# Output projections of a two-layer trunk by seven block products per pair of tiles, with weight sums made in DRAM

## The chip, the cores and the metric

One core of one Trainium2 chip runs the whole program. The metric is device time in microseconds (us) for one execution. The engines are named as in the profile: PE (matmul), PEld (weight load), DVE (vector), ACT (scalar), POOL (GpSimd) and SP, whose queue issues most of the DMAs.

## The reference

Two layers are computed over 16 learned meta tokens followed by 512 tokens, so 528 columns, with 1024 features. In each layer:

```python
h = rmsnorm(h_res, norm_gain[l])
proj = h @ w_in[l]        # u_pool, z_pool, c_q, c_kv, k_rope, z_mla, g_pool, g_mla
y_pool = (pool_mix(u_pool, ...) * silu(z_pool)) @ pool_w_up[l]
o_mla  = mla(c_q, c_kv, k_rope, pos, ...)          # latent attention, 8 heads
y_mla  = (o_mla * silu(z_mla)) @ mla_w_up[l]
merged = sigmoid(g_pool) * y_pool + sigmoid(g_mla) * y_mla
h_res  = h_res + merged @ w_out[l]
```

The output is `h_res` without the meta tokens. The change concerns the last line, a product of a 1024 x 1024 matrix with 1024 features by 528 columns (512 in the last layer, where the meta tokens are no longer needed).

## The kernel before

Activations are kept transposed: features on the 128 partitions, tokens along the free dimension. A matrix of 1024 outputs is worked in 8 tiles of 128 outputs, and the 1024 inputs of each tile in 8 blocks of 128. Every float32 operand is split into a high part in the rounded format float32r and a low remainder, and each block is three matmuls: high by high, low activation by high weight, and high activation by low weight (`mm3`, lines 184 to 187).

All plain projections stand in one list, `plan`, built by `register`. `stream` walks through it as a generator: it loads weights four chunks of 512 columns ahead (`wload`: SP loads a `raw` tile, of which there are three, ACT makes the high part `whi` on line 180, DVE the low part `wlo` on line 181), emits the matmuls, and calls an evacuation routine for each finished PSUM tile. The layer's own code, `go`, calls `upto(name)` to run the list as far as a named projection, and `gap` or `fill` to put a stretch of these matmuls between the steps of attention, so that PE has work while a head's softmax is on its way. After the program is written in this order, the tile framework's scheduler sets the final order on each engine.

In layer 0 a projection has two column segments of 264, in layer 1 one of 512. PSUM has four tiles `mm` for projections and three tiles `S`, which attention uses for its scores.

The stages around the change:

- `gm0` to `gm7`: the gates of the attention branch, kept in slots `cq0` to `cq7`.
- `mu0` to `mu7`: the up projection of the attention branch. `ev_mu` multiplies by the gate on DVE from PSUM (line 882), adds the pooling branch `am`, which lives in the tile `xb`, on POOL (line 884), and splits the sum into high and low on ACT and DVE (lines 276 and 277). The result is `mg[m]`, in the buffers `hh`/`hl` which also hold the normalised input of a layer.
- `o0` to `o7`: the output projection. `ev_o` loads the residual of the tile by SP, computes 0.5 x PSUM + residual on DVE (line 898), and stores it: to the output in the last layer, otherwise into `xb`, with a copy to the DRAM tensor `scr` (from which the last layer loads its residual) and a square for the next norm.
- After `o7` of layer 0, `split_h` makes the next layer's `hh`/`hl` from `xb` (lines 336 and 338).

The evacuation of the output projection before:

```python
sp.dma_start(xr[:, a:b], xT[:, m, a:b])
dve.scalar_tensor_tensor(out=xn[:, a:b], in0=ps, scalar=0.5, in1=xr[:, a:b], op0=ALU.mult, op1=ALU.add)
sp.dma_start(scr[:, m, a0 - NM:b - NM], xn[:, a0:b])
if b == T:
    nxt.square_x(m)
```

Of the kernel before, what the change touches and what calls it, by code (L numbers as in the profile page):

```python
# [9 lines left out]
F32 = mybir.dt.float32  # L10
# [61 lines left out]
def trunk(ctx, tc, xT, pos, win, wkr, wqb, wkb, wvb, wgr, wpu, wmu, wout, gains, const, yT):  # L72
# [44 lines left out]
    def rawt():  # L117
        return wp.tile([P, 512], F32, tag="raw", name=nm("raw"), bufs=3)
# [48 lines left out]

    loads = [0]
# [15 lines left out]
    def mm3(out, wh, wl, xh, xl, start, stop):  # L184
        pe.matmul(out, wh, xh, start=start, stop=False)  # L185
        pe.matmul(out, wh, xl, start=False, stop=False)  # L186
        newest[0] = pe.matmul(out, wl, xh, start=False, stop=stop)  # L187
# [5 lines left out]
    def stream():  # L193
# [3 lines left out]
        def load(i):  # L197
            g_, c = flat[i]
            n = min(512, g_.width - c)
            return wload(g_.src[:, c:c + n], n, g_.gain, g_.spare)  # L200
# [109 lines left out]

    hbuf = [(slot(f"hh{k}", F32R), slot(f"hl{k}", F32R)) for k in range(8)]

    class Layer:
        def __init__(self, l):
            self.l, self.last = l, l == DEPTH - 1
            self.XS = XTOK if self.last else FULL
            self.x0 = NM if self.last else 0
            self.xt = xt if l == 0 else [None] * 8
# [7 lines left out]
            self.sq = []  # L326
            self.st = self.acc = self.inv = self.cinv = self.kraw = self.kp = None
# [13 lines left out]
        def square_x(self, k):  # L341
            self.xsq[k] = slot(f"cq{4 + k}" if k < 4 else f"q{k}")
# [534 lines left out]
        def ev_mu(self, m):  # L877
            def ev(ps, a, b):
                if a == self.x0:
                    self.mg[m] = self.hs[m]  # L880
                t = tmp()
                dve.scalar_tensor_tensor(out=t[:, :b - a], in0=self.gms[m][:, a:b], scalar=1.0, in1=ps,  # L882
                                         op0=ALU.add, op1=ALU.mult)
                gp.tensor_add(t[:, :b - a], t[:, :b - a], self.am[m][:, a:b])  # L884
                split(*self.mg[m], t[:, :b - a], a, b)
            return ev

        def ev_o(self, m, nxt):
            def ev(ps, a, b):
                xr = tmp()  # L890
                if self.last:
                    sp.dma_start(xr[:, a:b], scr[:, m, a - NM:b - NM])
                    xn = xr
                else:
                    sp.dma_start(xr[:, a:b], xT[:, m, a:b])
                    nxt.xt[m] = xb[:, m]
                    xn = nxt.xt[m]
                dve.scalar_tensor_tensor(out=xn[:, a:b], in0=ps, scalar=0.5, in1=xr[:, a:b],
                                         op0=ALU.mult, op1=ALU.add)
                a0 = max(a, NM)  # L900
                if self.last:
                    sp.dma_start(yT[:, m, a - NM:b - NM], xn[:, a:b])
                    return
                sp.dma_start(scr[:, m, a0 - NM:b - NM], xn[:, a0:b])
                if b == T:
                    nxt.square_x(m)
            return ev

        def register(self, nxt):
# [52 lines left out]
            for m in range(8):  # L962
                add(f"mu{m}", wmu[l, m], 512, evac=self.ev_mu(m), xs=lambda: self.ogs, segs=XS)
                plan[-1].spare = m % 2 == 1
            mg = lambda: self.mg
            for m in range(8):
                add(f"o{m}", wout[l, m], D, evac=self.ev_o(m, nxt), xs=mg,
                    segs=[(NM, NM + SEQ // 2), (NM + SEQ // 2, T)] if self.last and m == 7 else XS)
# [4 lines left out]
        def go(self, nxt):  # L973
# [13 lines left out]
            self.norm_sums()  # L987
            up("u1")
# [22 lines left out]
            for h in range(H):  # L1011
# [4 lines left out]
                self.pv(prev, (2, 3))  # L1016
                prev = kn_
# [6 lines left out]
            self.pv(prev, (2, 3))  # L1024
            up("gm7")
            flush()
            if not self.last:
                for p in range(4):
                    self.meta_out(p)
            up("o7")  # L1030
# [79 lines left out]
```

## Time and profile before

| what | value |
|---|---|
| timed runs (median; lowest to highest of 3) | 789.21 us; 789.16 to 789.3 |
| profiled execution, first to last instruction (span) | 787.1 us |
| median of the timed runs less that span | 2.1 us |
| granted PE clock | 1.000 |
| PE, DVE, ACT, POOL busy in the span | 780.9, 535.1, 410.8, 194.4 us |
| `mu` and `o` of layer 0, first matmul to first matmul of what follows | 332.4 to 356.4, 356.4 to 403.3 us |
| `mu` and `o` of layer 1 | 716.6 to 739.1, 739.1 to 783.8 us |

The profile is of one execution. The span is what its instructions cover; no separate total is listed for that execution, so the median of the timed runs stands beside it. In the rows of the profile, a line such as "L181 DVE TENSOR_TENSOR wlo<-raw,whi" names the line of the kernel, the engine, the operation, and what it writes and reads by the program's names without buffer numbers. Matmuls overlap, so the duration of one is longer than the distance to the next.

### The profile page before, as it was taken

What the parts mean: (1) busy time and instruction counts of PE and PEld (TensorE: products, weight loads), DVE (VectorE), ACT (ScalarE), POOL (GpSimd) and SP (SyncE); (2) the same over time, 40 slices, a digit from 0 to 9 for tenths busy, and PEclk for the clock granted to TensorE, in tenths of its full rate; (3) what the DMA queues carried; (4) which work ended last, traced back from release to release, by engine and by line L of the source; (5) the groups of instructions that cost most, each with busy time, mean ns of one, the idle gap of its engine ahead of it and who ended that gap; (6) DMA issues with size and microseconds to landing.
All of it is one profiled execution on the core that took longest, in us unless ns stands there. A gap on an engine that the chain in (4) does not pass through costs nothing.

```text
span 787.1 us, 14567 instructions
## 1 busy us (share of the span) xinstructions
PE 780.9 (99%) x5301; PEld 708.6 (90%) x5301; DVE 535.1 (68%) x1165; ACT 410.8 (52%) x930; POOL 194.4 (25%) x259
## 2 busy tenths in 40 slices
PE   9999999999999999999999999999999999999998
PEld 8999899999999999999997898887788888887887
DVE  5848787446779987675464487775467888755932
ACT  7645655635656565633354356455445666554420
POOL 1034504002333242051000145131022333410500
PEclk9999999999999999999999999999999999999999
DMA  6242333423223212224642422334232222122372
GB/s 242 82 102 85 96 120 102 128 81 94 96 76 92 78 58 78 95 81 146 192 123 94 95 88 90 129 88 136 96 105 88 95 84 82 65 81 67 102 242 84
DMA packets 52263, 81.83 MB, mean 104 GB/s; under 512 B 8784, under 2 KB 17360, under 8 KB 52192
## 3 DMA queue, kind: packets, MB, share of 16 engines
q1 hardware_dynamic: 52048, 80.65, 32.9%
q8 instruction: 41, 0.67, 0.4%
q14 instruction: 30, 0.25, 0.1%
q10 hardware_dynamic: 144, 0.26, 0.1%
HBM read 74.49 MB, written 4.27 MB: 100 GB/s over the span
## 4 chain that ended last, share of the span: by engine, by line
PE 95%; DMA 2%; DVE 1%; issue 1%; ACT 0%; SPq 0%; ACTq 0%
PE mm L185 28%; PE mm L187 28%; PE mm L186 28%; PE mm L796 2%; PE S L186 2%; PE S L187 1%; PE S L185 1%; PE o L802 1%; PE o L801 1%; PE S L453 1%; DMA xb<-xT 1%; PE mm L355 1%; DVE wlo L181 1%; PE mm L412 0%; DMA rinv<-win 0%
## 5 line engine op out<-in xcount | busy, mean ns | idle before, releaser
L185 PE MATMUL mm<-hh,whi 128*128 128x264 f32 (+2 forms) x1096 | 346.7, 318 | 0.2 <-ACT racc L810 0.2
L186 PE MATMUL mm<-hl,whi 128*128 128x264 f32 (+2 forms) x1096 | 343.9, 315 | 0.0
L187 PE MATMUL mm<-hh,wlo 128*128 128x264 f32 (+2 forms) x1096 | 343.0, 315 | 0.0
L181 DVE TENSOR_TENSOR wlo<-raw,whi 128x512 fp32r<-128x512 f32 (+2 forms) x251 | 188.6, 755 | 119.6 <-ACT whi L180 115.9
L180 ACT ACTIVATE whi<-raw 128x512 fp32r<-128x512 f32 (+2 forms) x251 | 150.4, 601 | 187.5 <-PE mm L186 126.5
L185 PEld LDWEIGHTS mm<-hh,whi 128*128 128x128 f32 x1096 | 205.9, 188 | 13.6 <-ACT racc L810 0.5
L186 PEld LDWEIGHTS mm<-hl,whi 128*128 128x128 f32 x1096 | 206.6, 189 | 11.8
L187 PEld LDWEIGHTS mm<-hh,wlo 128*128 128x128 f32 x1096 | 205.5, 188 | 12.0
L774 POOL TENSOR_TENSOR pm<-pa,rs 128x16 f32<-128x16 f32 x32 | 11.6, 361 | 181.3 <-DVE rs L769 181.3
L560 POOL TENSOR_TENSOR racc<-racc,tmp 128x264 f32<-128x264 f32 (+1 forms) x15 | 14.2, 948 | 153.8 <-ACT tmp L559 129.8
L702 POOL TENSOR_TENSOR tmp<-kp,bc 64x528 f32<-64x528 f32 x16 | 22.5, 1408 | 76.9 <-PE mm L675 44.5
L884 POOL TENSOR_TENSOR tmp<-tmp,xb 128x264 f32<-128x264 f32 (+1 forms) x24 | 27.1, 1149 | 58.2 <-DVE tmp L882 33.1
L730 DVE CUSTOM_DVE_ANT_0 S<-S,maskw,nqs 128x272 f32<-128x272 f32 (+4 forms) x80 | 38.5, 498 | 4.2 <-PE S L187 3.9
L737 ACT ACTIVATE cq<-S,bia 128x400 f32<-128x400 f32 (+2 forms) x48 | 24.6, 516 | 22.6 <-DVE bia L764 12.0
L185 PE MATMUL mm<-u,whi 128*128 128x264 f32 (+1 forms) x108 | 35.2, 326 | 0.0
L187 PE MATMUL mm<-cq,wlo 128*128 128x264 f32 (+1 forms) x108 | 34.5, 323 | 0.7 <-DVE wlo L181 0.7
L187 PE MATMUL mm<-u,wlo 128*128 128x264 f32 (+1 forms) x108 | 34.8, 323 | 0.0
L185 PE MATMUL mm<-cq,whi 128*128 128x264 f32 (+1 forms) x108 | 34.6, 320 | 0.0
L186 PE MATMUL mm<-cq,whi 128*128 128x264 f32 (+1 forms) x108 | 34.5, 321 | 0.0
L277 DVE TENSOR_TENSOR tl<-mm,th 128x512 fp32r<-128x512 f32 (+1 forms) x64 | 29.3, 481 | 6.1 <-ACT th L276 5.1
L776 POOL TENSOR_TENSOR cq<-cq,rs 128x384 f32<-128x384 f32 (+1 forms) x32 | 32.8, 1025 | 0.0
L186 PE MATMUL mm<-kn,whi 128*128 128x264 f32 (+1 forms) x96 | 30.7, 321 | 0.0
(252 smaller groups left out, 1362.4 us busy)
## 6 DMA issues: line engine op xcount, KB each, us to landing
raw<-win SPq DMA_DIRECT2D x143, 256.0 KB, 2.6
raw<-wout SPq DMA_DIRECT2D x32, 256.0 KB, 2.7
bc<-kdr SPq DMA_DIRECT2D x16, 264.0 KB, 3.6
raw<-wpu SPq DMA_DIRECT2D x16, 256.0 KB, 2.7
raw<-wmu SPq DMA_DIRECT2D x16, 256.0 KB, 2.5
raw<-wqb SPq DMA_DIRECT2D x12, 256.0 KB, 2.6
tmp<-xT SPq DMA_DIRECT2D x16, 132.0 KB, 3.0
tmp<-scr SPq DMA_DIRECT2D x7, 256.0 KB, 3.4
```

Of the source, the lines that this page charges most:

```text
L180: act.activation(hi[:, :n], raw[:, :n], AF.Copy)
L181: dve.tensor_sub(lo[:, :n], raw[:, :n], hi[:, :n].bitcast(F32))
L185: pe.matmul(out, wh, xh, start=start, stop=False)
L186: pe.matmul(out, wh, xl, start=False, stop=False)
L187: newest[0] = pe.matmul(out, wl, xh, start=False, stop=stop)
L277: dve.tensor_sub(lo[:, a:b], src, hi[:, a:b].bitcast(F32))
L702: gp.tensor_mul(kf[r0:r0 + 64, :], self.kp[r0:r0 + 64, :], bc[r0:r0 + 64, :])
L730: dve.tensor_tensor_reduce(out=sv, in0=sv, in1=mask, scale=nqs[:, i, h:h + 1], scalar=3e38, op0=ALU.add, op1=ALU.min, accum_out=bia[:, c:c ...
L737: act.activation(pv, sv, AF.Exp, scale=-1.0, bias=bia[:, i:i + 1], accum_out=rs[:, c:c + 1])
L776: gp.tensor_mul(pt[i][:, NM:], pt[i][:, NM:], rs[:, i:i + 1].to_broadcast([P, n - NM]))
L796: pe.transpose(tr[:, P * (i - j):P * (i - j + 1)], pt[i][:, NM + P * j:NM + P * (j + 1)], ident)
L884: gp.tensor_add(t[:, :b - a], t[:, :b - a], self.am[m][:, a:b])
```

## The change

The output projection is done by Strassen's scheme in Winograd's form. The 1024 inputs are taken as two halves (tiles 0 to 3 and 4 to 7), the columns as two halves (`XH`: 264 and 264 in layer 0, 256 and 256 in layer 1), and the outputs as four pairs of tiles. For each pair, eight products of four blocks become seven, numbered `p` in the code: three use plain activations (`p` 1, 2, 3), four use mixed ones (4 to 7). Of the weights, three products take a plain half tile of `wout` and four take a sum, kept in a new DRAM tensor `wsum`.

- `ev_mu` keeps its result unsplit in `f`, makes high and low halves of what plain products need (`halves`, with the factor 0.5), and for each pair of tiles k and k + 4 `mixed` makes the activation sums on DVE and POOL and splits them.
- `weight_sums` is called once per head step: SP copies four half tiles from `wout` to `wsum` in DRAM, and POOL adds to them with accumulating DMAs. The first DMA of each group waits for the newest matmul.
- `residual` loads the residual into `xb` right after the `mu` of a tile; products are added there on DVE, or copied to SBUF by ACT and added by POOL where one product goes to several places.
- The order of products is written out in `out_body` (`head` + `rest`). The `mu` tiles go in the order 0, 4, 1, 5, 2, 6, 3, 7.
- The copy of layer 0's result to `scr` is written after `cq1` of layer 1. There are five `raw` tiles, and squares of layer 1 use other slots.

```diff
-        return wp.tile([P, 512], F32, tag="raw", name=nm("raw"), bufs=3)
+        return wp.tile([P, 512], F32, tag="raw", name=nm("raw"), bufs=5)
...
+    wsum = [[dp.tile([P, 4, 512], F32, name=f"wsum{l}{u}") for u in range(4)] for l in range(DEPTH)]
...
             def ev(ps, a, b):
-                t = tmp()
-                dve.scalar_tensor_tensor(out=t[:, :b - a], in0=self.gms[m][:, a:b], scalar=1.0, in1=ps,
-                                         op0=ALU.add, op1=ALU.mult)
-                gp.tensor_add(t[:, :b - a], t[:, :b - a], self.am[m][:, a:b])
-                split(*self.mg[m], t[:, :b - a], a, b)
+                t = self.f[m]
+                hi = T if m >= 4 else mid
+                for c, d in self.XH:
+                    if a <= c and d <= b:
+                        dve.scalar_tensor_tensor(out=t[:, c:d], in0=self.gms[m][:, c:d], scalar=1.0, in1=ps[:, c - a:d - a],
+                                                 op0=ALU.add, op1=ALU.mult)
+                        gp.tensor_add(t[:, c:d], t[:, c:d], self.am[m][:, c:d])
+                        if d == hi:
+                            self.halves(self.mg[m], t, self.x0, hi)
+                if b == T:
+                    if m >= 4:
+                        self.mixed(m - 4)
...
+        def halves(self, hl, t, a, b):
+            act.activation(hl[0][:, a:b], t[:, a:b], AF.Copy, scale=0.5)
+            dve.scalar_tensor_tensor(out=hl[1][:, a:b], in0=t[:, a:b], scalar=0.5, in1=hl[0][:, a:b].bitcast(F32),
+                                     op0=ALU.mult, op1=ALU.subtract)
+
+        def mixed(self, k):
...
+            dve.tensor_sub(w[:, b:c], u[:, b:c], w[:, b:c])
+            gp.tensor_sub(u[:, b:c], u[:, a:b], u[:, b:c])
+            dve.tensor_sub(u[:, a:b], u[:, a:b], w[:, b:c])
+            self.halves(self.tt[k][0:2], u, a, c)
+            gp.tensor_sub(w[:, a:b], w[:, a:b], u[:, a:b])
+            self.halves(self.tt[k][2:4], w, a, c)
...
+            head = [(p, u) for u in range(3) for p in (1, 3, 2)]
+            rest = [(6, 0), (5, 0), (7, 0), (6, 1), (4, 0), (5, 1), (7, 1), (6, 2), (4, 1), (5, 2), (7, 2), (1, 3), (4, 2),
+                    (6, 3), (2, 3), (5, 3), (7, 3), (3, 3), (4, 3)]
...
+                for k in range(4):
+                    xs = self.mg[k + o] if p < 4 else self.tt[k][o:o + 2]
+                    c = P * k
+                    mm3(ps, w[0][:, c:c + P], w[1][:, c:c + P], xs[0][:, a:b], xs[1][:, a:b],
+                        k == 0 and p not in (2, 7, 4), k == 3, True)
...
+                if p == 1:
+                    self.q1[u] = q = sqt()
+                    act.activation(q[:, :n], ps, AF.Copy)
+                    gp.tensor_add(x12, x12, q[:, :n])
+                    gp.tensor_sub(x22, x22, q[:, :n])
+                    gp.tensor_sub(x21, x21, q[:, :n])
+                elif p == 2:
+                    dve.tensor_add(x11, ps, x11)
+                    finish(m, A)
...
+        def weight_sums(self, h):
+            l = self.l
+            u, s = divmod(h, 2)
+            if u < 4:
+                a, b = wout[l, 2 * u], wout[l, 2 * u + 1]
+                d = wsum[l][u]
+                if s == 0:
+                    for i, t in enumerate((b[:, 0:512], a[:, 0:512], a[:, 0:512], a[:, 512:1024])):
+                        behind(sp.dma_start(d[:, i, :], t), newest[0])
+                else:
+                    behind(gp.dma_start(d[:, 0, :], b[:, 512:1024], accum_op=ALU.add), newest[0])
+                    behind(gp.dma_start(d[:, 2, :], b[:, 0:512], accum_op=ALU.add), newest[0])
+            if u > 0:
+                d = wsum[l][u - 1]
+                behind(gp.dma_start(d[:, 3 if s else 1, :], d[:, 1 if s else 0, :], accum_op=ALU.add), newest[0])
...
-            for m in range(8):
+            for i, m in enumerate((0, 4, 1, 5, 2, 6, 3, 7)):
                 add(f"mu{m}", wmu[l, m], 512, evac=self.ev_mu(m), xs=lambda: self.ogs, segs=XS)
...
+            if l > 0:
+                up("cq1")
+                for k in range(8):
+                    behind(sp.dma_start(scr[:, k, :], xb[:, k, NM:T]), newest[0])
...
                 self.pv(prev, (2, 3))
+                self.weight_sums(h)
...
-            up("o7")
+            for i, m in enumerate((0, 4, 1, 5, 2, 6, 3, 7)):
+                up(f"mu{m}")
+                self.residual(m)
+            up("o")
```

Lines of the changed kernel that are used below: matmuls of `mm3` stand on lines 191 to 193, the weight splits on 186 and 187, POOL's add of `ev_mu` on 901, and the low part of `halves` on 911.

More of the change, by code (lines that the diff above doesn't have):

```diff
@@ L199, in load @@
             n = min(512, g_.width - c)
-            return wload(g_.src[:, c:c + n], n, g_.gain, g_.spare)
+            return wload(g_.chunk(c, n), n, g_.gain, g_.second(c))
         ahead = []
@@ L961, in register @@
                 add(f"gm{m}", wi(MT_GM + m), D, evac=self.ev_gm(m), xs=hs, segs=XS)
-            for m in range(8):
+            for i, m in enumerate((0, 4, 1, 5, 2, 6, 3, 7)):
                 add(f"mu{m}", wmu[l, m], 512, evac=self.ev_mu(m), xs=lambda: self.ogs, segs=XS)
[L964 to L968, printed above, removed]
+                plan[-1].spare = i % 2 == 1
+            src, body = self.out_body(nxt)
+            add("o", src, 512 * len(src), body=body)
         def gap(self):
```

104 lines of the change are left out of this document (81 added, 23 removed).

## The prediction

> **What bounds the kernel now.** I read the page first, then stretches of the time line.
>
> ```profile
> span 787.1 us, 14567 instructions
> PE 780.9 (99%) x5301; PEld 708.6 (90%) x5301; DVE 535.1 (68%) x1165; ACT 410.8 (52%) x930; POOL 194.4 (25%) x259
> PEclk9999999999999999999999999999999999999999
> PE 95%; DMA 2%; DVE 1%; issue 1%; ACT 0%; SPq 0%; ACTq 0%
> ```
>
> PE is never idle, at full clock, and 95% of the chain that ends last is PE. A matmul taken away is worth its pitch, as long as nothing makes PE wait instead. So I look at who else is close to full in the two stages that the change touches: `mu` (which makes the operand of the output projection) and `o` (the projection itself). The next view gives busy time by stretch: `mu` and `o` of layer 0, `mu` and `o` of layer 1, and then, for each layer, the stretch from the first evacuation of `mu` to the last low half that `o` needs.
>
> ```profile
> core 0: us, PE busy (x) PEld busy (x) DVE busy (x) ACT busy (x) POOL busy (x), PEclk, DMA share, GB/s
> 332.40:356.40 24.00, 23.72 (x192) 23.51 (x193) 19.86 (x44) 10.63 (x25) 12.94 (x14) 1.00 0.24 80
> 356.40:403.30 46.90, 46.90 (x387) 46.90 (x386) 21.49 (x40) 17.85 (x31) 1.88 (x3) 1.00 0.57 171
> 716.60:739.10 22.50, 22.50 (x100) 18.29 (x99) 17.47 (x22) 10.26 (x17) 8.02 (x5) 1.00 0.28 83
> 739.10:783.80 44.70, 44.69 (x217) 37.18 (x215) 19.98 (x30) 10.01 (x16) 4.24 (x3) 1.00 0.49 159
> 338.20:360.00 21.80, 21.52 (x177) 21.31 (x176) 19.68 (x38) 10.59 (x23) 14.82 (x16) 1.00 0.24 80
> 726.80:747.20 20.40, 20.40 (x89) 16.55 (x88) 19.32 (x24) 9.54 (x16) 12.27 (x8) 1.00 0.29 92
> ```
>
> In `o` DVE and POOL have room (21.5 and 1.9 of 46.9 us). In the last two rows DVE is busy 90 and 95% while POOL is busy 68 and 60%: `mu` is the tight stage.
>
> **Matmuls saved.** From the time line, the first matmul of `o` in each layer, and the first and last of the 48 matmuls of 256 columns at the end:
>
> ```profile
> 356.41 0.28 PE L185 MATMUL mm<-hh,whi 128*128 128x264 f32 x1
> 739.11 0.39 PE L185 MATMUL mm<-hh,whi 128*128 128x512 f32 x1
> 777.95 0.28 PE L185 MATMUL mm<-hh,whi 128*128 128x256 f32 x1
> 783.51 0.28 PE L187 MATMUL mm<-hh,wlo 128*128 128x256 f32 x1
> ```
>
> Layer 0 has 8 tiles x 8 blocks x 3 x 2 segments = 384 matmuls of 264 columns in 46.9 us, a pitch of 0.122. The scheme needs 4 pairs x 7 products x 4 blocks x 3 = 336: 48 x 0.122 = 5.9 us less. Layer 1 takes 44.7 us now, mostly at 512 columns. After, it is 336 matmuls of 256 columns, whose pitch is (783.51 - 777.95)/47 = 0.118: 39.7 us, 5.0 less. Sum: **-10.9 us**, if PE never waits.
>
> **The sums of activations.** Three new steps per tile pair stand between `mu` and `o`: subtractions of half tiles (two on DVE, two on POOL for each of four pairs of blocks), and high and low halves of two mixed operands. What they cost depends on how DVE and POOL live together:
>
> ```profile
> L882 DVE SCALAR_TENSOR_TENSOR tmp<-cq,mm x16: 416/418/430, 338.3 to 357.7; 128x264 f32<-128x264 f32 x16
> L181 DVE TENSOR_TENSOR wlo<-raw,whi x6: 679/1331/1781, 728.0 to 738.6; 128x512 fp32r<-128x512 f32 x6
> L181 DVE TENSOR_TENSOR wlo<-raw,whi x11: 680/683/694, 749.6 to 775.8; 128x512 fp32r<-128x512 f32 x11
> L575 DVE SCALAR_TENSOR_TENSOR xb<-tmp,xb x4: 420/454/864, 262.2 to 274.3; 128x264 f32<-128x264 f32 x4
> L884 POOL TENSOR_TENSOR tmp<-tmp,xb x16: 743/880/1202, 338.8 to 358.3; 128x264 f32<-128x264 f32 x16
> L884 POOL TENSOR_TENSOR tmp<-tmp,xb x8: 1289/1678/1748, 727.6 to 743.7; 128x512 f32<-128x512 f32 x8
> ```
>
> (minimum/median/maximum in ns.) The weight split L181 reads two SBUF tiles: 0.68 us in `o`, up to 1.78 in `mu`, where POOL adds. L575 shows the same of a scalar_tensor_tensor with two SBUF tiles (0.42 to 0.86). L882, which reads PSUM, stays at 0.42 to 0.43. And POOL's add goes from 0.74 to 1.20, or 1.29 to 1.74. So a DVE operation with two SBUF tiles and a POOL operation take turns. Back to back, DVE's steps are shorter than their durations:
>
> ```profile
> 352.26 0.42 DVE L277 TENSOR_TENSOR hl<-tmp,hh 128x264 fp32r<-128x264 f32 x1
> 352.61 0.42 DVE L882 SCALAR_TENSOR_TENSOR tmp<-cq,mm 128x264 f32<-128x264 f32 x1
> 746.57 0.68 DVE L277 TENSOR_TENSOR hl<-tmp,hh 128x512 fp32r<-128x512 f32 x1
> 747.17 0.68 DVE L181 TENSOR_TENSOR wlo<-raw,whi 128x512 fp32r<-128x512 f32 x1
> 338.26 0.43 DVE L882 SCALAR_TENSOR_TENSOR tmp<-cq,mm 128x264 f32<-128x264 f32 x1 [3.08 <-PE mm L187]
> 726.79 0.69 DVE L882 SCALAR_TENSOR_TENSOR tmp<-cq,mm 128x512 f32<-128x512 f32 x1 [2.94 <-PE mm L187]
> ```
>
> 0.34 us for 264 columns (352.26 to 352.61), 0.60 for 512 (746.57 to 747.17), so an estimated 0.62 for 528 and 0.33 for 256. Now a test of "they take turns" on what is there. Layer 0, 338.3 to 360.0: 16 POOL adds x 0.74 + 16 L277 x 0.34 + 6 L181 x 0.60 = 20.9 us of turns in a stretch of 21.8. Layer 1, 726.8 to 747.2: 8 x 1.29 + 8 x 0.60 + 7 x 0.60 = 19.3 in 20.4. The pair is full now, and PE just escapes, since `o` can run some matmuls before it needs the last tile.
>
> [...]
>
> After, layer 0. The order of the changed program shows what stands in DVE's and POOL's queues up to the low half of tile 7, the last that PE's first products need. POOL: 16 adds + 3 + 2 subtractions, 21 x 0.74 = 15.5. DVE: 4 halves x 0.34, 9 halves x 0.62, 6 subtractions x 0.34, 8 weight splits x 0.60 = 13.8. Together 29.3 us from 338.3, so 367.6. PE reaches the matmul that reads it 33 matmuls into `o`: 356.4 + 33 x 0.122 = 360.4. **A stall of 7 us.** Tiles and weights of the products before it stand in the same queue, so the stall may come in pieces, and PSUM evacuations queue behind blocked DVE operations.
>
> After, layer 1. POOL 20 x 0.72 (0.743 x 256/264) = 14.4; DVE 4 x 0.33 + 8 x 0.60 + 5 x 0.33 + 10 x 0.60 = 13.8: 28.2 us from 726.8, so 755.0. PE wants it 43 matmuls into `o`: 739.1 + 43 x 0.118 = 744.2. **A stall of 10.8; I take 10**, since four of the weight splits stand so early that they may fall into DVE's pauses for PE.
>
> The bounds of both stalls: if DVE and POOL overlapped fully, DVE alone would need 13.8 + 16 evacuations x 0.34 = 19.2 us, to 357.5 and 746.0: 0 and 1.8 us of stall. If turns take 6% more: 9 and 12.5. I take values near the upper end, as the two stretches above do.
>
> **The rest of `o`.** Weight loads go from 16 to 28 a layer: 12 more splits x 0.60 on DVE and as many on ACT. DVE's 21.5 us in layer 0 become 21.5 - 16 x 0.34 + 12 x 0.60 + 27 evacuations x 0.34 + about 3 for the last mixed halves = 35 us, and POOL's 15 new adds (11 us) push it towards 46, against 41 us of matmuls. PE covers it only barely; bounds 0 and 5 us, I take 1 for both layers together. ACT (17.9 + some 11) is covered.
>
> **Sums of weights in DRAM.** 16 copies on SP's queue and 16 accumulating DMAs on POOL's queue per layer, most of them within the heads.
>
> ```profile
> POOL pm L774 <- DVE rs L769: 181.3, 16, 28.0
> 245.00:260.00 15.00, 15.00 (x125) 14.80 (x125) 12.75 (x33) 10.26 (x27) 2.58 (x4) 1.00 0.23 80
> 580.00:700.00 120.00, 120.00 (x625) 101.84 (x624) 96.39 (x220) 73.02 (x181) 38.88 (x62) 1.00 0.27 85
> L114 SPq DMA_DIRECT2D raw<-wout x32: 328/328/465, 340.2 to 768.4; - x32
> DMA to landing us min/median/max: 2.4/2.7/4.7
> 783.83 0.42 DVE L898 SCALAR_TENSOR_TENSOR tmp<-mm,tmp 128x256 f32<-128x256 f32 x1 [0.99 <-PE mm L187]
> ```
>
> The trace has no DMA from POOL. Nearest rows: SP's issue, 0.33 us, and a load's landing, 2.7, if POOL were held until then. 16 of them are 5 to 43 us of POOL in a layer's heads, where POOL is idle for 81 of 120 us and waits 181 us in all for DVE's reciprocals. DMA is 23 to 27% busy there. POOL's softmax products queue behind a DMA that waits for a weight sum or for PE, and PE's transposes behind those. On SP, the first copy of each group waits for the newest matmul, with four copies and then weight loads behind it; the loads run four ahead of PE (12 matmuls x 0.122 = 1.5 us for each segment, 11 to 12 us in all), which covers 1 MB of copies. Price of both queues: 0 to 4 us; less than nothing is excluded, since no work goes away there. I take 0, by the idle row. [...]
>
> **Moved transfers, with one answer each.** Residual loads move from the evacuations into `mu`, behind POOL's adds on SP, with weight loads behind them; loads run four chunks ahead as told, and five raw buffers instead of three keep that up, so 0. The eight writes of layer 1's residual move from `o` to after `cq1`: 2.1 MB ahead of weight loads, hidden by the same depth, 0 to 3 if it isn't enough; I take 0. At the end an evacuation (783.83, 0.42 us) and a half-tile store close the kernel as now: 0.
>
> **Sum.** -10.9 + 7 + 10 + 1 = +7.1 us on the span of 787.1. The three timed runs have a median of 789.21, 2.1 us over the span, which lie outside the first and last instruction and stay. **796.3 us.**
>
> **The rivals.**
> Forecast (0.52): turns of DVE and POOL make PE wait between `mu` and `o`; 796.3, by itself 791 to 801.
> Faster (0.23): the turns are shorter than my sum, at the start of each `o`. POOL's slowest add of 264 columns takes 1.20 us with a split of 0.60 in its way, where 0.74 + 0.60 = 1.34 would be expected: a tenth overlaps there. If 17% of all turns overlapped, the last low half would come at 338.3 + 24.3 = 362.6 and 726.8 + 23.4 = 750.2, stalls of 2.2 and 6.0: -10.9 + 8.2 + 1 gives 785.4. It decides from about 14% on, where the stalls fall below 9.9 together. For it: the 1.20, and a PE that never waits today with the pair already full. Against: both whole stretches took 4 to 6% more than the plain sum, not less.
> Even (0.08): stalls of 10 to 12 eat the gain; 789.2.
> Slower still (0.15): POOL's DMAs delay the heads, or weight loads of `o` come late (28 x 256 KB, plus stores and residuals, 11.5 MB in 40 us is 290 GB/s, where `o` now moves 159 to 171 at a DMA share of 0.49 to 0.57). 4 us of heads and 5 of `o` on top: 805.
> It doesn't do what it says (0.02): the weight sums are late when they are loaded, SP stands still and all loads behind it: over 800.
>
> **How the numbers follow.** A measurement can tell 0.2% (1.6 us) from no change. Slower: 0.52 + 0.15 + 0.02 = 0.69; same 0.08; faster 0.23. The range leaves out the best tenth (below 784) and the worst (above 804). The forecast's own 791 to 801 comes from stalls 5 us less or more in sum.
>
> **What would show it.** Right: 336 matmuls in each `o` at pitches of 0.122 and 0.118; PE idle before L193's matmuls at the start of `o`, released by DVE's L911 or by weight splits, some 7 and 10 us; L187, L911 and L901 at medians well over 0.68, 0.76 and 0.74 us in `mu`; heads of equal length. Wrong: PE without gaps there (then 779 to 786), or gaps in the heads before transposes that wait for POOL, or whi waiting for DMA in `o`.

## The result, and the profile after

The changed kernel takes 814.21 us (median of 4 runs, 813.01 to 815.94), the kernel before 789.18 on the same chip: a ratio of 1.0315, 95% interval 1.030 to 1.033. The forecast was 796.3 with a range to 804: the sign was right, the size was 18 us short. Later groups of runs had a median of 790.3 to 791.1 for the kernel before, so kernels are compared below by their ratio to it in the same group.

The page of the changed kernel, in four lines: span, busy time by engine, the granted clock in 40 slices, and the chain that ended last.

```profile
span 812.4 us, 15070 instructions
PE 783.9 (96%) x5373; PEld 715.3 (88%) x5373; DVE 590.2 (73%) x1246; ACT 434.3 (53%) x976; POOL 270.7 (33%) x345
PEclk9999999999999999989999999999999999999699
PE 86%; DVE 7%; DMA 2%; issue 2%; ACT 1%; POOL 1%; ACTq 0%; DVEq 0%; POOLq 0%
```

PE is no longer without gaps, DVE has 7% of the chain where it had 1%, and the clock string, all nines before, has an 8 and a 6, in the two `o` stages.

Where the time went shows in the starts of three matmuls: the first of `mu` in layer 0, the first of 512 columns in layer 1, and the first of `mu` in layer 1. Time line of PE, the kernel before, then the changed one:

```profile
332.36 0.39 PE L185 MATMUL mm<-q,whi 128*128 128x264 f32 x1
414.96 0.40 PE L185 MATMUL mm<-hh,whi 128*128 128x512 f32 x1
716.58 0.39 PE L185 MATMUL mm<-q,whi 128*128 128x512 f32 x1
```

```profile
331.89 0.28 PE L191 MATMUL mm<-q,whi 128*128 128x264 f32 x1
422.60 0.50 PE L191 MATMUL mm<-hh,whi 128*128 128x512 f32 x1 [2.04 <-ACT q L416]
724.05 0.39 PE L191 MATMUL mm<-q,whi 128*128 128x512 f32 x1
```

From the first to the second, which holds `mu` and `o` of layer 0, 82.6 us became 90.7: 8.1 more. From the second to the third, the heads, 301.6 became 301.5. From the third to the end, `mu` and `o` of layer 1, 70.5 became 88.3: 17.8 more. The matmuls saved are 5.9 and 5.0, so 14 and 23 us were lost, 37 in all, where 18 were forecast.

What PE waited for in `mu` and `o` of the changed kernel, first layer 0, then layer 1 (us in total, times, longest):

```profile
PE mm L191 <- DVE xb L999: 2.6, 1, 2.6
PE S L192 <- DVE hl L911: 2.0, 1, 2.0
PE S L193 <- DVE wlo L187: 1.4, 1, 1.4
PE mm L193 <- DVE wlo L187: 0.7, 1, 0.7
PE S L191 <- ACT hh L910: 0.5, 1, 0.5
...
PE S L192 <- DVE hl L911: 3.5, 1, 3.5
PE S L191 <- ACT whi L186: 3.2, 1, 3.2
PE S L193 <- DVE wlo L187: 2.2, 1, 2.2
PE S L191 <- ACT hh L910: 1.8, 2, 1.3
PE mm L191 <- DVE xb L993: 1.5, 1, 1.5
PE mm L191 <- DVE xb L999: 0.7, 1, 0.7
PE S L191 <- DVE xb L982: 0.5, 1, 0.5
```

The low halves (L911), weight splits (L187) and ACT's high halves (L910) are the wait that was forecast, from the start of `o` on: 4.6 us in layer 0, 7.5 in layer 1. The evacuations L993 and L999 and the late whi come in the second half of `o`, 2.6 and 5.4 us, and a wait of 2.04 stands at layer 1's norm (in the row at 422.60). With the rest that is some 23 us of idle time. The other part of the loss is in matmuls that run slower. Windows of the changed kernel (us, busy us and instructions of PE, PEld, DVE, ACT and POOL, granted clock, DMA share, GB/s): 

```profile
358.00:360.00 2.00, 0.82 (x7) 0.61 (x5) 2.00 (x4) 0.00 (x0) 1.56 (x2) 1.00 0.19 53
362.00:364.00 2.00, 0.64 (x3) 0.60 (x3) 2.00 (x3) 1.77 (x4) 1.95 (x2) 0.50 0.08 29
364.00:366.00 2.00, 2.00 (x11) 2.00 (x11) 2.00 (x3) 1.02 (x3) 1.65 (x2) 0.50 0.66 144
368.00:370.00 2.00, 2.00 (x19) 2.00 (x18) 2.00 (x3) 0.74 (x2) 2.00 (x2) 1.00 0.46 125
340.00:376.00 36.00, 31.75 (x234) 30.52 (x232) 35.66 (x50) 18.16 (x36) 30.23 (x30) 0.91 0.52 153
732.00:776.00 44.00, 35.71 (x186) 31.16 (x185) 41.16 (x58) 19.33 (x39) 34.29 (x35) 0.84 0.43 133
```

During a wait that begins in 358 to 360 the granted clock falls to 0.50, at 360.1, and stays there for 6.8 us. PE, busy all the time in 364 to 366, has 11 matmuls in that row, where the row of 368 to 370, at full clock, has 19. The trace has one more such stretch in layer 0 and three in layer 1, of 3.4 or 6.8 us each. Matmul steps longer than their pitch add up to 4.7 us in layer 0 and 8.0 in layer 1; of these some 3.5 and 6 us lie in the slow stretches (an estimate: 36 and 63 matmuls start there, each about 0.1 us longer), and the rest are first steps behind a wait and gaps in the record. This term was not in the forecast at all. The last two rows show who sets the pace: DVE is busy 35.66 of 36 us and 41.16 of 44, beside a POOL at 30 and 34, from the first evacuations of `mu` to far into `o`. In these 36 us DVE gets only 50 instructions done. Their durations, from 335 to 380 us, by groups (busy us, mean ns):

```profile
L187 DVE TENSOR_TENSOR wlo<-raw,whi 128x512 fp32r<-128x512 f32 x16 | 17.6, 1114 | 0.0
L899 DVE SCALAR_TENSOR_TENSOR u<-cq,mm 128x264 f32<-128x264 f32 x8 | 3.4, 420 | 2.2 <-PE mm L193 2.2
L901 POOL TENSOR_TENSOR u<-u,xb 128x264 f32<-128x264 f32 x8 | 8.9, 1112 | 5.7 <-DVE u L899 5.7
L979 POOL TENSOR_TENSOR xb<-xb,sq 128x264 f32<-128x264 f32 x3 | 3.6, 1206 | 0.0
```

A weight split that takes 0.68 us by itself takes 1.11 on average; POOL's sums, 0.74 at best before, take 1.11 and 1.21 in the two groups shown, 0.90 to 1.21 in all of them; the operation that reads PSUM keeps its 0.42.

### The profile page after: what moved, and what is told of

Its sections match the earlier page's. It is cut to its first block, busy times and chain, and to the rows that moved or that the text cites. A ratio compares the mean times of both kernels' runs of the same rounds, so it can differ in the third digit from the quotient of the medians.

```text
span 812.4 us, 15070 instructions
## 1 busy us (share of the span) xinstructions
PE 783.9 (96%) x5373; PEld 715.3 (88%) x5373; DVE 590.2 (73%) x1246; ACT 434.3 (53%) x976; POOL 270.7 (33%) x345
## 4 chain that ended last, share of the span: by engine, by line
PE 86%; DVE 7%; DMA 2%; issue 2%; ACT 1%; POOL 1%; ACTq 0%; DVEq 0%; POOLq 0%
PE mm L191 24%; PE mm L193 23%; PE mm L192 23%; PE S L192 3%; PE S L193 3%; PE S L191 3%; DVE wlo L187 2%; PE mm L808 2%; DVE hl L911 1%; PE o L814 1%; PE o L813 1%; DMA raw<-wsum 1%; PE S L465 1%; PE mm L367 1%; ACT whi L186 1%
## 5 line engine op out<-in xcount | busy, mean ns | idle before, releaser
L187 DVE TENSOR_TENSOR wlo<-raw,whi 128x512 fp32r<-128x512 f32 (+2 forms) x275 | 216.1, 791 | 107.1 <-ACT whi L186 103.4
L191 PE MATMUL mm<-hh,whi 128*128 128x264 f32 (+1 forms) x896 | 283.7, 318 | 2.3 <-ACT q L416 2.0
L192 PE MATMUL mm<-hl,whi 128*128 128x264 f32 (+1 forms) x896 | 280.9, 314 | 0.0
L193 PE MATMUL mm<-hh,wlo 128*128 128x264 f32 (+1 forms) x896 | 279.9, 315 | 0.0
L191 PEld LDWEIGHTS mm<-hh,whi 128*128 128x128 f32 x896 | 168.1, 188 | 13.5 <-ACT q L416 2.2
L192 PEld LDWEIGHTS mm<-hl,whi 128*128 128x128 f32 x896 | 168.6, 188 | 9.3
L193 PEld LDWEIGHTS mm<-hh,wlo 128*128 128x128 f32 x896 | 167.7, 188 | 9.9
L191 PE MATMUL mm<-cq,whi 128*128 128x264 f32 (+2 forms) x236 | 72.2, 307 | 4.8 <-DVE xb L999 3.3
L193 PE MATMUL mm<-cq,wlo 128*128 128x264 f32 (+2 forms) x236 | 71.4, 306 | 1.4 <-DVE wlo L187 1.4
L192 PE MATMUL mm<-cq,whi 128*128 128x264 f32 (+2 forms) x172 | 52.7, 308 | 0.0
L191 PEld LDWEIGHTS mm<-cq,whi 128*128 128x128 f32 x236 | 45.9, 194 | 6.8 <-ACT whi L186 2.8
L193 PEld LDWEIGHTS mm<-cq,wlo 128*128 128x128 f32 x236 | 45.4, 193 | 3.6 <-DVE wlo L187 2.0
```

The costliest lines, as they stand in the source:

```text
L187: dve.tensor_sub(lo[:, :n], raw[:, :n], hi[:, :n].bitcast(F32))
L191: pe.matmul(out, wh, xh, start=start, stop=False, skip_group_check=more)
L192: pe.matmul(out, wh, xl, start=False, stop=False, skip_group_check=more)
L193: newest[0] = pe.matmul(out, wl, xh, start=False, stop=stop, skip_group_check=more)
```

## The experiments

The theory at this point: DVE and POOL take turns, and the sum of their turns, not one late tile, sets the pace from 338 to 380 us and from 727 to 778. Rivals: the slow clock adds to the end by itself; weight loads of `o` are late; the order of the work is at fault; the sums in DRAM cost something.

**The sums in DRAM alone**, added to the kernel before:

```
+                self.weight_sums(h)      # in each head, 16 copies and 16 accumulating DMAs per layer
```

> The kernel before, with the sums of weights in DRAM added (32 copies on SP, 32 accumulating DMAs on POOL) and nothing reading them. Theory (the sums cost nothing, as predicted; from layer 1's first matmul of 512 columns to the first of mu, the two traces have 301.6 us before and 301.5 after): 789.2, within 1 us. Rival (they delay the heads and the gain of something else hides it): 791 to 793.

Measured: 0.999 of before (0.998 to 1.000). They cost nothing that can be seen. What they take of POOL's queue shows in the changed kernel, by groups:

```profile
L1025 POOL DMA_DIRECT2D wsum<-wsum x16 | 16.8, 1051 | 33.1 <-PE mm L193 19.3 <-PE mm L808 9.3 <-PE o L814 4.5
L1022 POOL DMA_DIRECT2D wsum<-wout x8 | 9.0, 1120 | 0.0
L1021 POOL DMA_DIRECT2D wsum<-wout x8 | 6.8, 853 | 27.8 <-PE mm L808 12.3 <-PE o L813 8.3 <-DMA raw<-win 7.2
```

32.6 us for 32 DMAs, 1.02 us each, and POOL isn't held until they land, 7.0 to 7.7 us later (medians).

**No sums of activations:**

```
     def mixed(self, k):
-        ... two subtractions on DVE, two on POOL, four halves
+        self.tt[k] = list(self.mg[k + 4]) * 2
```

> The changed kernel without the sums of activations: products 4 to 7 read the halves of tiles 4 to 7 instead of mixed operands, so the 8 subtractions per layer on DVE, the 8 on POOL and the 16 halves are left out; all loads, products and evacuations stay. Theory (the sums and the turns of DVE and POOL make PE wait, and everything else, late loads and lost clock, follows from that): PE keeps its saved 10.9 us but for 1 to 3 us, 779 to 782, clock 1.00. Rival (weight loads of o come late by themselves: 28 loads and 28 splits instead of 16): the gaps late in o stay, 2.7 us in layer 0 and 5.0 in layer 1 with some 3 us of lost clock behind them, 787 to 790.

This kernel leaves out the mixed operands, so products 4 to 7 are not those of the scheme. Measured: 791.8 us, 1.0015 (0.9997 to 1.0033). By the ratio that is 790.4 where the kernel before takes 789.2: far from the theory, and just above the rival, by which the loads and splits of `o` are enough to hold PE. The sums are worth 24 us, but even without them PE loses what it saves. It loses it in layer 1: from `mu` to `mu` layer 0 is 4.5 us shorter than before, and the rest is 6.6 longer where 5.0 of matmuls are saved.

**POOL's work on DVE**, in three parts: the sums of `mu`, the residual sums of products 1 and 3, and both.

```
-                        gp.tensor_add(t[:, c:d], t[:, c:d], self.am[m][:, c:d])
+                        dve.tensor_add(t[:, c:d], t[:, c:d], self.am[m][:, c:d])
...
-                    act.activation(q[:, :n], ps, AF.Copy)
-                    gp.tensor_add(x12, x12, q[:, :n])
+                    dve.tensor_add(x12, ps, x12)
```

> The changed kernel with POOL's sums in mu (16 or 8 adds and 8 subtractions per layer) moved to DVE, nothing else. Theory (DVE and POOL take turns, so POOL's 0.74 us blocks DVE as long): a sum of 264 columns costs 0.34 on DVE instead of 0.74 on POOL. Layer 0 up to the low half of tile 7: 13.8 + 21 x 0.34 + 16 evacuations x 0.34 = 26.3 us instead of 29.3; layer 1 25.7 instead of 28.2. Some 3 us less at the start of each o and less clock lost: 803 to 809. Rival (DVE is simply full, and POOL works beside it): DVE gets 24 x 0.34 + 16 x 0.34, about 7 us more per layer: 822 to 828.

> The changed kernel with only the residual sums of products 1 and 3 moved (15 per layer from POOL, 1.1 to 1.2 us each there, to DVE straight from PSUM, without ACT's copies); POOL's sums of mu stay. Moving mu's sums alone took 3.9 us off, moving both 14.5. Theory (turns: each POOL sum blocks DVE for its own length, and these stand in the stretch where DVE never pauses): 15 x (0.74 - 0.34) = 6 us of turns per layer, 8 to 12 us in all: 802 to 806, 1.017 to 1.022 of before. Rival (the two moves help only together, since POOL must be empty): 809 to 814.

> As the run with POOL's sums of mu on DVE, and the residual sums of products 1 and 3 (15 per layer on POOL from an SBUF copy that ACT makes) on DVE straight from PSUM, without the copies. Theory (turns): 15 x 0.74 = 11 us of POOL's turns become 15 x 0.34 = 5 us of DVE, in the stretch where DVE is busy without a pause: 3 to 6 us better than the run with only the sums of mu moved, 798 to 805. Rival (DVE is simply full): 5 us per layer on top, over 825.

Measured: 1.0248 (1.0225 to 1.0272), 1.0142 (1.0126 to 1.0157) and 1.0104 (1.0077 to 1.013). The sums of `mu` are worth 5 us, the residual sums 14, both 17: more work for a DVE that is full already makes the kernel faster, and a DVE that is full by itself is excluded. The residual sums are the larger part though they are fewer, 15 against 24 per layer. What moves in all three is the length of DVE's other work. Weight splits in `o` of layer 1, the changed kernel, then with the residual sums on DVE:

```profile
L187 DVE TENSOR_TENSOR wlo<-raw,whi 128x512 fp32r<-128x512 f32 x12 | 13.1, 1114 | 0.0
```

```profile
L187 DVE TENSOR_TENSOR wlo<-raw,whi 128x512 fp32r<-128x512 f32 x15 | 12.2, 830 | 1.2 <-ACT whi L186 1.2
```

The same splits in a fixed stretch, 340 to 376 us of layer 0, follow POOL step by step (POOL's busy time, mean of one split):

| kernel | POOL, us of 36 | split, us |
|---|---|---|
| as changed | 30.2 | 1.13 |
| residual sums on DVE | 20.4 | 0.95 |
| sums of `mu` on DVE | 14.2 | 0.83 |
| both on DVE | 0.0 | 0.69 |

The times don't follow in the same order. In layer 0 moving the sums of `mu` gained nothing (the table further down has 8.7 us against 7.9), though the splits became shorter; DVE's own added work is the likely reason. The residual sums had more to give: on DVE they read PSUM and take 0.42 us (L976 to L978 of the run with both moved), as L899 does, and ACT's 15 copies and the step through POOL went with them. How much of the 14 us belongs to which of these, no run separates.

**The splits of `o` off DVE** (in the changed kernel, with POOL as it is):

```
-        dve.tensor_sub(lo[:, :n], raw[:, :n], hi[:, :n].bitcast(F32))
+        act.activation(lo[:, :n], raw[:, :n], AF.Copy)      # weights of o only
```

> The changed kernel, but the low halves of o's weights are copies of the raw weights made by ACT; the subtraction on DVE that makes them is left out (28 per layer, 1.11 us each in turns with POOL in the first 45 us, 0.68 without). All loads, sums, products and evacuations stay. Theory (the throughput of DVE with POOL's turns sets the pace from mu's evacuations on): some 15 us of turns go from the 40 us stretch of each layer; the waits of PE shrink by more than half: 790 to 800, 1.001 to 1.014 of before. Rival (the chain of the sums sets it: evacuation, POOL's add, subtractions, halves, each waiting for the one before): 808 to 815.

This kernel leaves out the low halves of these weights; copies of the raw weights stand in their place. Measured: 1.0089 (1.0058 to 1.0121), 18 us less than the changed kernel. The chain of the sums has the same steps as before; what went is the amount of DVE's work.

**PE kept busy in its waits:**

```
+                    if (l, i, k) in FILLERS:      # 72 matmuls of 128 columns on constants
+                        keep_busy(FILLERS[l, i, k])
```

> The changed kernel with 72 matmuls of 128 columns on constants (some 0.2 us each, result unused) put into PE's queue where its longest waits in o were, so that PE is busy there. Theory A (after a wait of some 2 us the granted clock falls to 0.5 for 4 to 8 us, 12.7 us of slow matmuls in all, and that adds to the end): with PE kept busy the clock stays near 1 and 8 to 12 us go: 802 to 806. Rival B (DVE's queue sets the pace in these stretches, and a slow PE only waits less at the next gap): clock near 1, PE waits longer elsewhere, 810 to 816.

Measured: 814.26 us, 1.0304 (1.0285 to 1.0322), as the changed kernel. The clock at the start of both `o`, changed kernel, then with fillers:

```profile
356.00:372.00 16.00, 12.15 (x77) 11.31 (x76) 16.00 (x21) 7.74 (x16) 13.03 (x13) 0.79 0.45 129
747.00:770.50 23.50, 15.21 (x73) 13.44 (x72) 22.86 (x31) 9.85 (x20) 20.05 (x21) 0.71 0.40 121
```

```profile
356.00:372.00 16.00, 10.32 (x78) 9.50 (x77) 15.29 (x21) 7.09 (x16) 11.27 (x12) 0.97 0.44 123
748.50:772.00 23.50, 18.12 (x127) 17.26 (x126) 22.75 (x33) 10.43 (x21) 18.43 (x19) 0.85 0.34 101
```

The clock rises from 0.79 to 0.97 and from 0.71 to 0.85, DVE is nearly as full as before, and the end doesn't move: at this pace a faster PE only waits longer for DVE. The fillers can delay PE too (layer 0 became 2.3 us longer, layer 1 2.4 shorter), so a small share of the clock isn't excluded; for 8 us the fillers would have to cost as much as the clock gave. The run with the sums of `mu` on DVE says the same: its mean clock is 0.996 against 0.983, and it is only 5 us faster.

**Loads of `o` earlier** (on the run without sums of activations):

```
+            for j in range(i + 1, min(i + 4, len(flat))):
+                pre[j] = fetch(...)      # three chunks earlier on SP's queue
```

> The run without sums of activations again (it leaves out the mixed operands, and measured 791.8, 1.0015 of before, not 779 to 782), with each weight load of o issued three chunks earlier on SP's queue, the splits where they were. What is open: why PE still loses 11 us of its saved 10.9 there. Theory (lead: a chunk now feeds 12 matmuls of 256 or 264 columns, 1.4 us instead of 2.8, so four chunks ahead are 5.7 us; on SP a load stands behind the store or residual of the product before, and then needs 3.3 us to land, 0.64 for whi, 0.69 for wlo): the gaps late in o (1.6 us in layer 0; 0.5, 2.8 and 0.7 in layer 1) and the lost clock behind them go: 0.993 to 0.996 of before, 784 to 787 on a chip where before takes 789.2. Rival (DMA is out of bandwidth, 28 loads of 256 KB and stores and residuals in 40 us): the gaps stay, 1.000 to 1.003 of before.

Measured: 1.0027 (1.0008 to 1.0046), against 1.0015: nothing. But the edit didn't do on the chip what it was for: counted from the start of `mu`, all loads of `o` but the first two of each layer were issued within 0.6 us of where they were. SP's loads wait for DVE to free a raw buffer (SP's waits, 752 to 768 us). So neither late loads nor DMA bandwidth is tested by this run:

```profile
SPq L114 <- DVE wlo L188: 4.1, 5, 1.4
```

The chain of waits of the changed kernel names the case, in order of time (start, us, what):

```profile
782.31 3.51 DMA raw<-wout
...
785.92 0.64 ACT whi L186
...
786.61 0.46 PE S L191
```

PE stands at product 1 of the last pair. The scheduler put it ahead of products that the program has earlier, but its load stands in SP's queue behind those products' loads (paired by the order of the program), and PE waits for it until 786.61.

**Another order**, without POOL: mixed operands of the last two block pairs and the residual sums of product 1 behind the low half of tile 7, all 12 products without mixed operands first; and the same with earlier loads.

```
-            head = [(p, u) for u in range(3) for p in (1, 3, 2)]
+            head = [(p, u) for u in range(4) for p in (1, 3, 2)]
...
+                behind(one, self.low)      # sums of pairs 2 and 3 after tile 7's low half
```

> The run without POOL (799.65, 1.0104 of before), with the order changed: the mixed operands of the last two pairs of blocks and product 1's residual sums stand behind the low half of tile 7 in DVE's queue, and the three products of the last tile pair that need no mixed operands come fourth instead of last (12 products, 17 us, before the first mixed one, instead of 9). Theory (order: the low half that PE's first products wait for stands behind sums that are not needed for 10 us): 5 us of idle at the start of each o and lost clock in layer 1, some 12 us in all, shrink to 3 to 6: 0.997 to 1.003 of before, 787 to 792. Rival (throughput: DVE is busy without a pause for 36 us from mu's evacuations on, so PE waits as long, only later): 1.008 to 1.012, 796 to 800.

> The run before it, with the weight loads of o three chunks earlier on SP's queue as in the first run of this call. Theory (lead): 2 to 4 us less than without, the late gaps go; if both theories hold, 0.993 to 0.999 of before, 784 to 789, the first of these kernels below the kernel before. Rival (DMA bandwidth, or DVE's throughput): no difference to the run before it within 1 us.

Measured: 1.0113 (1.0094 to 1.0132) and 1.0093 (1.0077 to 1.011), against 1.0104 without the new order. This order doesn't help, and the loads moved by little again, at most 1.2 us. The longest wait of PE in layer 1 is now one for a bank, whose residual sums stand behind the low half:

```profile
PE S L191 <- DVE xb L979: 3.8, 1, 3.8
```

**Neither POOL nor sums** (that order, and the mixed operands left out as above):

> The kernel without POOL and with product order changed (799.3, 1.0113 of before), and without the sums of activations: products 4 to 7 read the halves of tiles 4 to 7, so 16 subtractions and 16 halves per layer are left out. What is open: the run without these sums, but with POOL's adds, still lost 11 us of the saved 10.9. Theory (what was left there is POOL's turns, 31 adds per layer of mu and of the residual, and the product of the last tile pair that stands ahead of its weight load): 0.987 to 0.992 of before, 779 to 783 where before takes 789.2. Rival (the scheme's loads are enough to hold PE: a weight split for every 1.4 us of matmuls instead of every 2.8): PE still waits for wlo at the start of o, 0.996 to 1.002.

Measured: 0.9937 (0.9921 to 0.9954), between the two expectations. From mu to mu layer 0 is 5.6 us shorter than before, nearly all of its 5.9; layer 1, from mu to the end, is 2.3 us longer instead of 5.0 shorter. Windows of `o` in both layers:

```profile
355.40:396.00 40.60, 40.57 (x333) 40.35 (x332) 35.38 (x72) 23.71 (x39) 0.00 (x0) 1.00 0.62 182
733.00:780.30 47.30, 43.45 (x337) 41.83 (x335) 37.11 (x80) 16.60 (x27) 0.00 (x0) 0.96 0.61 183
```

In layer 0 PE is busy throughout at full clock. In layer 1 it isn't, for the same products. A likely reason, which no run tests by itself: there a chunk of weights fed 512 columns at once before, and feeds 256 after, while DVE still works off `mu`.

**Low halves made early** (that order, without POOL): 8 per layer made in the heads, stored, and loaded in `o`.

```
+            sp.dma_start(wlow[self.l][i], raw)      # in the heads
...
+            sp.dma_start(lo[:, :n].bitcast(F32), low)      # in o, instead of the split
```

> The kernel without POOL and with the product order changed (1.0113 of before), and the low halves of 8 weight chunks per layer (products 1 and 2) made in the heads, kept in DRAM and loaded straight into place in o: 8 splits less on DVE in the full stretch, 8 loads, splits and stores more in the heads, 8 loads of 256 KB more in o. Theory (DVE's throughput): 8 x 0.60 = 4.8 us of the full stretch of each layer go: 789 to 794 where before takes 789.2, 1.000 to 1.006. Rival (the loads of the low halves come late, or the heads pay): 1.010 to 1.020.

Measured: 1.0956 (1.091 to 1.100), the heads pay. Waits, PE's and SP's:

```profile
PE mm L194 <- ACT whi L186: 37.1, 12, 6.6
SPq L1021 <- DVE raw L1020: 33.6, 7, 10.4
```

Each store waits on SP for DVE's split, up to 10.4 us, and weight loads of the heads stand behind it in SP's queue. From `mu` of layer 1 to the end it takes 79.5 us, as the run with the same order and no early low halves (79.4): there PE waited for low halves and evacuations while DVE now had short pauses, so this run doesn't speak for the amount of DVE's work. It left open whether amount or waits decide.

**Residual sums later** (the new order, no POOL): ACT's copies free the banks, DVE adds them behind the last mixed operand.

```
+                    act.activation(q[:, :n], ps, AF.Copy)
+                    behind(dve.tensor_add(x12, x12, q[:, :n]), self.ready)
```

> The kernel without POOL and with the product order changed (1.0113 of before), where ACT copies products 1 and 3 out of PSUM and DVE adds them to the residual only behind the last mixed operand, so PE's banks come free early and 15 sums (5 us) per layer leave the stretch in which DVE never pauses. Theory (the amount of DVE's work ahead of the last mixed operand, and banks that wait for it): 4 to 5 us per layer less, 790 to 793 where before takes 789.2, 1.001 to 1.005. Rival (a wait elsewhere takes its place, as when the low halves were made early: the work is only moved, and splits and evacuations behind it come late): 1.009 to 1.013.

**The scheme in layer 0 alone**, with that, and as in the change:

```
+            if self.last:
+                ... the eight block products of the kernel before
```

> The version with the late residual sums in layer 0, and the old projection of eight block products in layer 1. Theory (each layer's cost stands by itself, and in layer 0, where a chunk of weights before the change feeds two segments of 264 columns and the matmuls saved are 5.9 us, nearly all can be kept, as the run without sums shows, 5.6 of 5.9): 784 to 788 where before takes 789.2, 0.994 to 0.998. Rival (layer 0 keeps losing what it loses in the version with the product order alone, 1.6 us from mu to mu): 790 to 791.5, 1.001 to 1.003.

> The changed kernel's layer 0 and the old projection in layer 1, nothing else. Theory (each layer's cost stands by itself): from mu of layer 0 to mu of layer 1 the trace of the changed kernel is 7.9 us longer than before, and the rest, 17.8, goes with layer 1: 796 to 798, 1.009 to 1.012 of before. Rival (layer 1's loss comes in part from layer 0, through transfers or sums of weights that run late): 800 to 806.

Measured: 1.0052 (1.0038 to 1.0065); **0.9964 (0.9951 to 0.9976)**, 787.27 us where the kernel before takes 790.25, the only complete version that is faster than it; and 1.0095 (1.008 to 1.0111). All three fall on the side of their theory, the first at its edge. So each layer's cost stands by itself, to about 1 us. The first run took sums out of the full stretch and freed the banks early at once, so it doesn't tell amount and banks apart. The stretch from 340 to 376 us in the version for layer 0, which is the row to set beside 50 instructions above:

```profile
340.00:376.00 36.00, 33.79 (x272) 33.07 (x271) 35.84 (x85) 20.21 (x40) 0.00 (x0) 1.00 0.57 166
```

DVE is as full, 35.84 of 36 us, but gets 85 instructions done without POOL beside it, where it got 50, and PE 272 matmuls at full clock instead of 234. The instructions aren't all the same; the weight splits among them are, 13 at 1.13 us on average in the changed kernel and 16 at 0.69 here.

The two parts of each kernel, against before, from the starts of `mu` as above (us):

| kernel | `mu` 0 to `mu` 1 | `mu` 1 to end |
|---|---|---|
| as changed | +7.9 | +17.8 |
| that with fillers | +10.3 | +15.4 |
| no sums of activations | -4.5 | +6.6 |
| splits of `o` off DVE | +1.6 | +8.3 |
| sums of `mu` on DVE | +8.7 | +13.3 |
| residual sums on DVE | +3.6 | +8.7 |
| no POOL | +2.3 | +9.0 |
| no POOL, new order | +1.6 | +8.9 |
| residual sums later | -2.3 | +7.7 |
| that, layer 0 alone | -1.6 | -0.1 |
| as changed, layer 0 alone | +6.7 | -0.2 |
| no sums, no POOL | -5.6 | +2.3 |

## Why the prediction was wrong, point by point

**Matmuls saved, -10.9: right in layer 0, not seen in layer 1.** With neither POOL nor the sums, 5.6 of layer 0's 5.9 us were there. Layer 1's 5.0 never showed: every version of it was longer than before.

**Turns of DVE and POOL, +7 and +10: right in mechanism and place, and near in idle time** (4.6 and 7.5 from the start of `o` on, by L911 and L187 as told). The traces show the turns by the operands: in 340 to 376 us a split, with two SBUF inputs, went from 1.13 us beside a POOL busy for 30.2 of the 36 us to 0.69 beside a POOL at 0.0, and L899, one of whose inputs is in PSUM, took 0.42 us in both. What makes the two engines take turns, no run shows.

**The rest of `o`, +1 with bounds 0 and 5: this step failed.** The prediction added DVE's 35 us and POOL's 11 for layer 0, 46 against 41 us of matmuls, and still took 1 for both layers. It also began that sum with empty queues at the first matmul of `o`, and gave layer 1, where each chunk of weights serves half as many columns as before, no sum of its own. The runs show a far larger term. DVE comes out of `mu` with a backlog and has hardly a pause until 382 us. Taking the 15 residual sums off POOL gave back 14 us, all of POOL's work 17, the splits of `o` off DVE 18, the sums of activations 24 (they overlap, so these don't add). With the sums of activations left out, layer 0 loses 1.4 us of the 5.9 that it saves, as the term had it, but layer 1 loses 11.6, part of it at the start of `o`, and 7.3 without POOL as well.

The working had stopped at the low half of tile 7, the first of several deadlines. The last mixed operand and the weight splits behind it are later ones in the same queue. The prediction's own sum, carried on to the last mixed operand of layer 0, is 36 POOL sums x 0.74 = 27 us and 21 us of DVE's two-input work, 48 us from 338.3: 386. PE, which needs it in product 7, after 11 products of 1.46 us, would be there at 372.5. In the trace the operand is ready at 378.6, so this sum is some 7 us long, an overlap of 15%; even so it comes 6 us behind a PE that had not been held up before. The PE of the trace had been: it came to its first mixed product at 374.1, and waited 0.7 us there, for a split.

**Missing: the granted clock.** It goes to 0.50 around the waits, for 3.4 or 6.8 us at a time. Some 9.5 us of longer matmuls lie in these stretches. The fillers show that most of this runs while PE would wait for DVE anyway, so it is more a part of how the loss looks than of its cause. PE had not stood idle for the whole 3.41 us ahead of the fall at 360.1: it was busy for 1.61 of them, and its longest wait there had lasted 1.3 us. How long a wait has to be for the clock to fall, no run shows.

**Sums of weights in DRAM, 0: right,** by a run with nothing else changed and by heads of 301.5 us. POOL's 1.02 us for each, 16 us per layer where the prediction had 5 to 43, lie within its idle time: with layer 1's among its work it is busy for 91.2 of the 300 us from 424 to 724.

**Moved transfers, 0: not borne out.** The late waits, 2.6 and 5.4 us, were not among the terms. The longest, 3.2, is a product that stands before its load's turn; in the 2.6 an evacuation stands behind a split that waits for its load. Both are orders inside queues. The two loads took 3.5 and 3.7 us to land, where 2.7 was the median before, so bandwidth may have a part of up to 1 us in each.

**The end, 0: right;** 3.5 us from the last matmul's start to the end of the span, 3.6 before.

**Rivals.** "Slower still" came nearest in size, 805, and that was luck: its 4 us of heads weren't there, and its 5 us of late loads are near the 3.2 and 2.6 us of waits above, which have another cause as far as shown. The faster rival's 785.4 is a span; with the 2.1 us that the forecast adds, its own sum gives 787.5. What it asked for, shorter turns, was there in part (the 15% above) and didn't decide.

Still open: why layer 1 keeps 7.7 us with the late residual sums and 2.3 even without sums. Its windows say that DVE is full at the start of `o` while splits are wanted twice as often, but no run halved them there by itself; the run that took them off DVE had the sums and POOL's work in place and still lost 8.3 us. Whether loads issued earlier would help is open too.

## What to carry to other kernels

A new step's operations have to be priced in the queue of the engine that is full, up to the last deadline in that queue and not only the first; work beside a stretch of matmuls is covered by it only if the two engines beside it can work at once, which DVE's splits and POOL's sums did only in small part here (1.13 us for a split with POOL busy for 30.2 of 36 us, 0.69 with POOL at 0.0). Where DVE operations with two SBUF inputs and POOL sums share a stretch, moving POOL's work onto a full DVE can shorten it, as the residual sums did here, by 14 us; the sums of `mu`, 5 us, did so in one layer only. A change that saves matmuls twice can be worth keeping once: in the layer whose stages have room.

## What the runs showed that was not expected

DVE got 85 instructions done in 36 us without POOL and 50 with it, busy all the time in both; the rows of busy time alone don't tell them apart, means of a single instruction do. The granted clock fell by half for 6.8 us during a wait of 2.0 us, at 360.1, and was raised again, from 0.79 to 0.97 and from 0.71 to 0.85 at the starts of `o`, by 72 matmuls of filling without any effect on the end, 814.21 against 814.26 us. A wait of the same length didn't always bring it down. In this trace the slow stretches begin and end a multiple of 3.41 us apart (360.10, 366.93, 387.41, 390.82), as if the time were cut into stretches of that length. In the one ahead of each fall PE was busy for 0.2 to 1.6 us of 3.41. The wait of 2.04 us at layer 1's norm falls on two of them, and PE was busy for 2.4 us in each; behind it the changed kernel has

```profile
424.00:428.00 4.00, 4.00 (x19) 3.24 (x18) 0.69 (x1) 0.63 (x1) 0.00 (x0) 1.00 0.23 67
```
